# Gates spread over the partitions by way of DRAM, and an output projection begun earlier, in a two-layer diffusion step

## Chip, cores and metric

The kernel runs on one core of a Trainium2 chip. The metric is the device time of one execution in microseconds (us). Engines are named as in the profile: PE is TensorE (PEld its weight load), DVE VectorE, ACT ScalarE, POOL GpSimd, SP SyncE, which here only issues DMAs. A trailing q (SPq, ACTq, POOLq) is an engine's DMA issue.

## What is computed

One step of a trunk of two layers over 128 context and 512 latent tokens of width 1024. Layer 0 mixes with gated grouped-query attention, layer 1 with a bidirectional gated linear recurrence of 8 heads (HGRN2). Both end in an output projection, an adaLN gate and a LayerNorm:

```
mod = silu(cond) @ ada_w[i] + ada_b[i];  shift, scale, g = split(mod, 3)    # one set for context, one for latent tokens
h = x * (1 + scale) + shift
if i == 0: out = gated attention(h) @ attn_w_out
else:      out = (rms_norm(o) * norm_gain * silu(gate path)) @ rec_w_out     # o from the two scans of the recurrence
x = layer_norm(ALPHA * x + g * out, ln_gain[i], ln_bias[i])
```

Here g is one vector of 1024 numbers for the context tokens and one for the latent tokens, in each layer. Outputs are both token streams, the new key and value cache, and the recurrence's final states.

## The kernel before

*Numbers.* Most projections split each fp32 operand into two fp32r parts, hi and lo, and sum three products (hi·hi, hi·lo, lo·hi). A weight comes in pieces of 128x1024 (512 KB). `split_piece` makes hi by an ACT cast (L218) and lo by a subtraction (L219), here mostly on DVE. The raw pieces come through a ring of three buffers that SP loads in the order of the list `order` (L207); SP works in order, so a load that waits for a buffer holds those behind it.

*Stages.* Layer 0's attention takes the time to about 360 us. A scheduler (`weave`, with a timeline of its own) interleaves score and softmax blocks (`sc`, `pscp`, `p`, `pt`, `pot`) with side work: query projections (`qmm`, `qps`), and the adaLN products (`ada_gen`). For each chunk of 256 columns of ada_w, `ada_mms` sums over two raw pieces on PE (tile `adaps`, L261), DVE copies the row (L267), `ada_out` turns it into columns by four small matmuls (L275), and DVE adds the bias (L282). For a gate chunk that gives the tile `gcol`. `spread` then puts it on all partitions: four fp32 matmuls of a column, repeated along the free axis, against the identity (L291, tile `gateps`, eight instructions in the trace), and a DVE copy (L292) into `gate[layer]`. There are four such chunks for each layer. Layer 0's are spread as they come; layer 1's columns wait in `gcol1` for the tail. Then come layer 0's output projection (weights `attn_w_out`) and LayerNorm.

*Layer 1*, from about 440 us on: for head h, `proj_gen` projects v and g (`vgps`) and then q and the two forget gates (three groups `rps`, L1108 to L1110), while a `Lane` interleaves `gla_gen` of the head before, by due times. `gla_gen` runs seven levels (tile `lv`, L1238 and L1244; DVE products L1247 and L1252 and ACT copies `kc` L1216 and `near` L1254 between them), then `kp`, `sp`, `op`, a normalization (L1309 to L1315), the transposes `oT` (L1320) and the split of the head's output into `ghi` (ACT, L1321) and `glo` (DVE, L1322). POOL carries `x1a`, layer 0's output with gain and bias, as the residual.

*Tail.* After the last projection `tail_gen` is woven with the last head's `gla_gen` by `SIDE_T`: it splits the 8 pieces of rec_w_out one by one (order `OUT1`: both column halves nh of piece 0, then of piece 1, and so on), spreads one gate chunk for each pair, and begins output tiles 0 and 1 with the heads k that are done. `out_mms` makes three matmuls 128x512 for each token tile, half and k, 240 in all (tile `outp`, L993 to L995). `Norm` then finishes each of the 5 token tiles: y = outp·gate (L1013, reads a half as soon as it is complete), residual (L1014), statistics (L1015, L1020), 1/sqrt on POOL (L189), and two passes with gain and bias (L1029, L1030), each half stored on SP or ACT. Both halves of a tile lie in one pair of banks, so the first matmul of half 1 of a tile that was not begun early is held until DVE has read half 0.

Of the kernel before, what the change touches and what calls it, by code (L numbers as in the profile page):

```python
# [18 lines left out]
P = 128  # L19
# [112 lines left out]
def hybrid_step(ctx: ExitStack, tc: tile.TileContext, a: dict, o: dict):  # L132
# [137 lines left out]
    def ada_out(layer, c, row):  # L270

        part, c4 = divmod(c, 4)
        ps = bank1("adaps2")
        for j in range(2):
            nc.tensor.matmul(ps[:, 2 * j:2 * j + 2], row[:, j * P:(j + 1) * P], sel, start=True, stop=True)  # L275
        src = ps[:, :4].rearrange("p (a b) -> p a b", a=2)
        bias = view(adab, (layer * 3 + part) * KT + 2 * c4, [[1, 2], [0, 2]])
        if part < 2:
            nc.vector.tensor_tensor(shsc[layer][:, part, 2 * c4:2 * c4 + 2, :], src, bias, ALU.add)
            return None  # L280
        gcol = gcol1[:, c4] if layer else tiny.tile([P, 2, 2], F32, tag="gc", name="gcol")[:]
        nc.vector.tensor_tensor(gcol, src, bias, ALU.add)  # L282
        return None if layer else lambda: spread(layer, c4, gcol)

    def spread(layer, c4, gcol):

        ps = bank1("gateps")
        for s in range(2):
            for j in range(2):
                col = bass.AP(gcol.tensor, gcol.offset + 2 * j + s, [list(gcol.ap[0]), [0, P]])  # L290
                nc.tensor.matmul(ps[:, (2 * s + j) * P:(2 * s + j + 1) * P], col, ident, start=True, stop=True)  # L291
        nc.vector.tensor_copy(gate[layer][:, :, c4 * CW:(c4 + 1) * CW], ps[:].rearrange("p (a b) -> p a b", a=2))  # L292

    def ada_gen(chunks):
        todo, last = None, None
        for l, c in chunks:
            ps = bank1("adaps")
            ada_mms(ps, l, c, 0)
            ada_mms(ps, l, c, 1)
            if last:  # L300
                last()
            last = todo and ada_out(*todo)
            yield
            todo = (l, c, ada_row(ps))
        if last:
            last()
        if todo:
            last = ada_out(*todo)
            yield
            if last:  # L310
                last()
                yield

# [659 lines left out]
    weave(att, side, SIDE_B)  # L973
    side.finish()
    modA, modB = h1_mod()
    ph.close()
# [12 lines left out]
    def out_mms(ps, tt, nh, ghi, glo, ks=range(KT)):  # L989
        t = slice(tt * P, (tt + 1) * P)  # L990
        for k in ks:
            hi, lo = wo[nh, k // 2]
            nc.tensor.matmul(ps[:, nh, :], ghi[:, k, t], hi[:, k % 2, :], start=(k == 0), stop=False)  # L993
            nc.tensor.matmul(ps[:, nh, :], ghi[:, k, t], lo[:, k % 2, :], start=False, stop=False)  # L994
            nc.tensor.matmul(ps[:, nh, :], glo[:, k, t], hi[:, k % 2, :], start=False, stop=(k == KT - 1))  # L995

    class Norm:
        def __init__(self, layer, tt, ps=None):
            self.layer, self.tt = layer, tt
            self.ps = bank2("outp") if ps is None else ps  # L1000
            if layer == 0:
# [7 lines left out]
        def half(self, nh):  # L1009
            s = slice(nh * 512, (nh + 1) * 512)  # L1010
            y = self.y[:, s]
            g = gate[self.layer][:, 1 if self.tt == TS else 0, s]
            nc.vector.tensor_tensor(y, self.ps[:, nh, :], g, ALU.mult)  # L1013
            nc.vector.scalar_tensor_tensor(y, self.x[:, s], ALPHA, y, ALU.mult, ALU.add)  # L1014
            nc.vector.bn_stats(self.st[:, nh, :], y)  # L1015
# [47 lines left out]
    def proj_gen(h, H, first):  # L1063
# [94 lines left out]
        tiles()  # L1158
        evac_vg()
        for i in range(3):  # L1160
# [165 lines left out]
    class Residual:  # L1326
# [19 lines left out]
        def step(self):  # L1346
# [6 lines left out]
            for _ in range(2):  # L1353
                if self.todo and not (self.live and self.todo[0][1] == 0):
                    self.load(*self.todo.popleft())

    residual = Residual()
    for h in range(RH):
# [8 lines left out]

    outs = {}

    def tail_gen():  # L1370

        gate[1] = g2.tile([P, 2, D], F32, tag="A", name="gate1")
        w1 = gsp.tile([P, 2, 1024], F32R, tag="gate", name="w1")
        slots = [w1[:, i, :] for i in range(2)]
        for _ in range(2):
            slots += [wr.tile([P, 1024], F32R, tag=t, name=t)[:] for t in ("whi", "wlo")]
        for tt in range(2):
            outs[tt] = bank2("outp")
        for n, (nh, i) in enumerate(OUT1):
            if n == 3:  # L1380
                w2 = gsp.tile([P, 5, 1024], F32R, tag="gs", name="w2")
                w3 = h1p.tile([P, 5, 1024], F32R, tag="h1lo", name="w3")
                slots += [t[:, i, :] for t in (w2, w3) for i in range(5)]
            hi, lo = slots[2 * n], slots[2 * n + 1]
            wo[nh, i] = tuple(t.rearrange("p (k n) -> p k n", k=2) for t in (hi, lo))
            split_piece(hi, lo, ("rec_w_out", nh, i), nc.vector)
            yield
            if nh == 0:
                continue
            spread(1, i, gcol1[:, i])  # L1390
            yield
            for tt in range(2):
                for k in (2 * i, 2 * i + 1)[:2 if i < 3 else 1]:
                    for nh in range(2):
                        out_mms(outs[tt], tt, nh, ghi, glo, [k])
                    yield

    xp = lpool("xp", 3)
# [18 lines left out]
    for tt in range(TT):  # L1417
        norm = Norm(1, tt, outs.get(tt))
        for nh in range(2):
# [81 lines left out]
```

## Time and profile before

| | us |
|---|---|
| runs | 887.34, 887.74, 892.66 (median 887.74) |
| the profiled execution | 883.77, of which the span is 881.9 |
| PE busy in the span | 837.9 (95%) |
| DVE, ACT, POOL busy | 538.7, 374.1, 203.1 |
| last rps matmul begins | 789.24 |
| last outp matmul begins | 871.80 |

A row of the timeline gives start, length, engine, line, operation, out<-in, shape and count; the bracket is the idle time of the engine before it and what ended that. The windows give busy time and (xcount) for PE, PEld, DVE, ACT and POOL, then the granted PE clock, the DMA engines' busy share and GB/s. The rows on DMAs end with the KB of one and the median time from issue to landing. In a chain row, the middle number is the row's share of the path.

### The profile page before, as it was taken

What the parts mean: (1) busy time and instruction counts of PE and PEld (TensorE: products, weight loads), DVE (VectorE), ACT (ScalarE), POOL (GpSimd) and SP (SyncE); (2) the same over time, 40 slices, a digit from 0 to 9 for tenths busy, and PEclk for the clock granted to TensorE, in tenths of its full rate; (3) what the DMA queues carried; (4) which work ended last, traced back from release to release, by engine and by line L of the source; (5) the groups of instructions that cost most, each with busy time, mean ns of one, the idle gap of its engine ahead of it and who ended that gap; (6) DMA issues with size and microseconds to landing.
All of it is one profiled execution on the core that took longest, in us unless ns stands there. A gap on an engine that the chain in (4) does not pass through costs nothing.

```text
span 881.9 us, 19250 instructions
## 1 busy us (share of the span) xinstructions
PE 837.9 (95%) x8116; PEld 744.0 (84%) x8116; DVE 538.7 (61%) x972; ACT 374.1 (42%) x735; POOL 203.1 (23%) x250
## 2 busy tenths in 40 slices
PE   5999999989999998999999999999999999989995
PEld 3689998878878766788899999999999999987783
DVE  2456534664645657576437486676767585758495
ACT  2133536534554767422343453544434444444200
POOL 2013001422323733010000223243333224110110
PEclk9999999999999999999999999999999999998998
DMA  9922122143141136441131323231322323132121
GB/s 312 371 88 84 49 71 74 49 144 97 49 145 49 49 122 213 145 142 72 37 117 50 109 73 97 64 123 51 103 85 85 97 70 102 53 113 100 55 96 71
DMA packets 32678, 89.86 MB, mean 102 GB/s; under 512 B 4400, under 2 KB 11568, under 8 KB 32592
## 3 DMA queue, kind: packets, MB, share of 16 engines
q1 hardware_dynamic: 21984, 71.57, 24.6%
q0 software_dynamic: 3984, 12.13, 5.0%
q10 hardware_dynamic: 6624, 4.93, 1.8%
q8 instruction: 64, 1.05, 0.5%
q14 instruction: 22, 0.18, 0.1%
HBM read 79.44 MB, written 9.18 MB: 100 GB/s over the span
## 4 chain that ended last, share of the span: by engine, by line
PE 86%; DVE 4%; DMA 4%; ACT 2%; issue 1%; POOL 0%; SPq 0%; DVEq 0%; ACTq 0%; POOLq 0%
PE rps L1108 7%; PE rps L1109 6%; PE rps L1110 6%; PE vgps L1098 5%; PE vgps L1099 4%; PE vgps L1100 4%; PE outp L993 4%; PE outp L994 4%; PE outp L995 4%; PE pot L750 4%; PE pt L832 3%; PE adaps L261 2%; PE lv L1238 2%; PE gps L317 2%; PE gps L318 2%; PE gps L319 2%
## 5 line engine op out<-in xcount | busy, mean ns | idle before, releaser
L1108 PE MATMUL rps<-h1hi,rhi 128*128 128x320 f32 x368 | 118.2, 321 | 0.0
L1109 PE MATMUL rps<-h1lo,rhi 128*128 128x320 f32 x368 | 115.0, 312 | 0.0
L1110 PE MATMUL rps<-h1hi,rlo 128*128 128x320 f32 x368 | 113.9, 310 | 0.0
L825 POOL TENSOR_SCALAR p<-p,rc 128x640 f32<-128x640 f32 x64 | 53.4, 838 | 79.3 <-DVE rc L824 77.5
L1108 PEld LDWEIGHTS rps<-h1hi,rhi 128*128 128x128 f32 x368 | 69.8, 190 | 1.3
L1109 PEld LDWEIGHTS rps<-h1lo,rhi 128*128 128x128 f32 x368 | 69.3, 188 | 0.0
L1110 PEld LDWEIGHTS rps<-h1hi,rlo 128*128 128x128 f32 x368 | 69.3, 188 | 0.0
L219 DVE TENSOR_TENSOR rlo<-raw,rhi 128x1024 fp32r<-128x1024 f32 x32 | 46.0, 1441 | 34.3 <-ACT rhi L218 34.3
L820 ACT ACTIVATE p<-sc,nm 128x640 f32<-128x640 f32 x64 | 51.0, 799 | 30.9 <-DVE nm L817 23.2
L817 DVE TENSOR_REDUCE nm<-sc 128x1 f32<-128x640 f32 x64 | 52.1, 818 | 17.1 <-PE sc L724 16.7
L1266 POOL COPY At<-near 32x160 f32<-32x160 f32 x32 | 14.0, 438 | 198.1 <-DVE near L1228 197.1
L1216 ACT COPY kc<-A 128x640 f32<-128x640 f32 x40 | 32.1, 804 | 57.4 <-DVE A L1247 50.3
L218 ACT CAST rhi<-raw 128x1024 fp32r<-128x1024 f32 x32 | 33.5, 1048 | 50.5 <-PE rps L1109 47.6
L1098 PE MATMUL vgps<-rhi,h1hi 128*128 128x256 f32 x180 | 51.5, 286 | 1.2 <-ACT h1hi L948 1.2
L832 PE MATMUL pt<-small,p 128*128 128x128 f32 x320 | 49.1, 278 | 2.6 <-ACT pts L728 0.8
L1100 PE MATMUL vgps<-rhi,h1lo 128*128 128x256 f32 x180 | 50.9, 283 | 0.4 <-DVE h1lo L949 0.4
L1099 PE MATMUL vgps<-rlo,h1hi 128*128 128x256 f32 x180 | 50.9, 283 | 0.0
L728 ACT COPY pts<-pt 128x512 f32<-128x512 f32 x64 | 36.4, 586 | 28.2 <-PE pt L832 27.4
L723 PE MATMUL sc<-kk,X 128*128 128x320 f32 x128 | 43.0, 345 | 3.8 <-ACT p L820 3.3
L832 PEld LDWEIGHTS pt<-small,p 128*128 128x128 f32 x320 | 37.5, 143 | 8.2 <-issue 5.5
L1098 PE MATMUL vgps<-wspare,h1hi 128*128 128x256 f32 x140 | 41.7, 298 | 0.0
L317 PE MATMUL gps<-hhi,whi 128*128 128x320 f32 x128 | 40.0, 313 | 0.4 <-ACT X L576 0.4
(263 smaller groups left out, 2401.4 us busy)
## 6 DMA issues: line engine op xcount, KB each, us to landing
raw<-in_ada_w SPq DMA_DIRECT2D x48, 512.0 KB, 4.8
raw<-in_rec_w_in SPq DMA_DIRECT2D x40, 512.0 KB, 3.7
raw<-in_attn_w_in SPq DMA_DIRECT2D x16, 512.0 KB, 4.5
raw<-in_attn_w_out SPq DMA_DIRECT2D x8, 512.0 KB, 4.5
raw<-in_rec_w_out SPq DMA_DIRECT2D x8, 512.0 KB, 3.6
x1d<-y SPq DMA_DIRECT2D x5, 512.0 KB, 2.6
rx<-x1d POOLq DMA_DIRECT2D x20, 128.0 KB, 3.8
x1a<-rx POOLq DMA_DIRECT2D x20, 128.0 KB, 2.8
```

Of the source, the lines that this page charges most:

```text
L219: (lo_eng or nc.gpsimd).tensor_tensor(lo, raw, hi.bitcast(F32), ALU.subtract)
L317: nc.tensor.matmul(ps[:, :320], w.hi(k)[:, c], hhi[:, k, t], start=(k == 0), stop=False)
L817: nc.vector.tensor_reduce(nm[:, 0:1], sc[:, :, :320], AX.XY, ALU.max, negate=True)
L820: nc.scalar.activation(halves(p[:]), sc[:, :, :320], AF.Exp, bias=nm[:, 0:1], accum_out=su[:, 0:1])
L825: nc.gpsimd.tensor_scalar(p, p, rs[:, 0:1], 1.0, ALU.mult, ALU.mult)
L832: nc.tensor.transpose(pt[:, i * 256 + q * P:i * 256 + (q + 1) * P], ps[q][:, (k0 + i) * P:(k0 + i + 1) * P], ident)
L1098: nc.tensor.matmul(out, h1hi[:, k, t], hi, start=(k == 0), stop=False)
L1099: nc.tensor.matmul(out, h1hi[:, k, t], lo, start=False, stop=False)
L1100: nc.tensor.matmul(out, h1lo[:, k, t], hi, start=False, stop=(k == KT - 1))
L1108: nc.tensor.matmul(ps[:, j, :320], hi[:, k, :], h1hi[:, k, t], start=(k == 0), stop=False)
L1109: nc.tensor.matmul(ps[:, j, :320], hi[:, k, :], h1lo[:, k, t], start=False, stop=False)
L1110: nc.tensor.matmul(ps[:, j, :320], lo[:, k, :], h1hi[:, k, t], start=False, stop=(k == KT - 1))
```

## The change

1. The gate columns of both layers stay in `gcol[layer]`. `gate_rows` writes them as two rows of 1024 numbers to DRAM, and `load_gate` loads each row onto all 128 partitions (512 KB each). Layer 0: written after the second query unit, loaded in the third, on SP. Layer 1: written on SP after attention, loaded on POOL's queue ahead of the residual tiles. All `spread` matmuls and their DVE copies are gone.
2. `order` has the first piece of rec_w_out ahead of the last piece of rec_w_in. `Tail.split` splits the first two pieces inside the last head's projection, and tiles 0 and 1 take k = 0 and 1 of half 0 right behind its last rps matmul.
3. The rest of the tail follows the list `PLAN`, one entry for each step of the last head's `gla_gen`: "s" is a split, (tt, k) are both halves of tile tt with head k. Tile 2 is begun early too.
4. `out_mms` and `Norm` take a list with a view for each half; tiles 3 and 4 use two separate bank pairs, one for each half.

```diff
-    gcol1 = const.tile([P, 4, 2, 2], F32, name="gcol1")
+    gcol = [const.tile([P, KT, 2], F32, name=f"gcol{i}") for i in range(2)]
...
-        gcol = gcol1[:, c4] if layer else tiny.tile([P, 2, 2], F32, tag="gc", name="gcol")[:]
-        nc.vector.tensor_tensor(gcol, src, bias, ALU.add)
-        return None if layer else lambda: spread(layer, c4, gcol)
-
-    def spread(layer, c4, gcol):
-
-        ps = bank1("gateps")
+            return
+        nc.vector.tensor_tensor(gcol[layer][:, 2 * c4:2 * c4 + 2, :], src, bias, ALU.add)
+
+    def gate_rows(layer):
+
         for s in range(2):
-            for j in range(2):
-                col = bass.AP(gcol.tensor, gcol.offset + 2 * j + s, [list(gcol.ap[0]), [0, P]])
-                nc.tensor.matmul(ps[:, (2 * s + j) * P:(2 * s + j + 1) * P], col, ident, start=True, stop=True)
-        nc.vector.tensor_copy(gate[layer][:, :, c4 * CW:(c4 + 1) * CW], ps[:].rearrange("p (a b) -> p a b", a=2))
+            nc.sync.dma_start(gated[layer][s].rearrange("(k p) -> p k", p=P), gcol[layer][:, :, s])
+
+    def load_gate(layer, queue):
+        for s in range(2):
+            queue.dma_start(gate[layer][:, s, :], gated[layer][s:s + 1, :].to_broadcast((P, D)))
...
+    gated = [dram.tile([2, D], F32, name=f"gated{i}") for i in range(2)]
...
-    order.extend(("rec_w_out", nh, i) for nh, i in OUT1)
+    order.insert(len(order) - 1, ("rec_w_out", *OUT1[0]))
+    order.extend(("rec_w_out", nh, i) for nh, i in OUT1[1:])
...
         yield from q_gen(c, Xs[c], ada_gen(ADA_B[c - 1]))
+        if c == 1:
+            gate_rows(0)
+        elif c == 2:
+            load_gate(0, nc.sync)
...
     side.finish()
+    gate_rows(1)
...
+            ps = bank2("outp") if ps is None else ps
+            self.ps = [ps[:, 0, :], ps[:, 1, :]] if not isinstance(ps, list) else ps
...
         for i in range(3):
+            if last and i == 2:
+                tail.split()
             if i:
                 load_q(i)
             yield from mms(i, 0)
+            if last and i == 2:
+                tail.split()
             yield from mms(i, 1)
+            if last and i == 2:
+                tail.fill(0, 0, (0, 1))
+                tail.fill(1, 0, (0, 1))
             evac(i)
...
+        def fill(self, tt, nh, ks):
+            if tt not in self.outs:
+                ps = bank2("outp")
+                self.outs[tt] = [ps[:, 0, :], ps[:, 1, :]]
+            out_mms(self.outs[tt], tt, nh, ghi, glo, ks)
...
+    PLAN = (["s"], [(0, 2), "s"], [(1, 2), "s"], [(0, 3), (1, 3), "s"], [(0, 4), "s"], [(1, 4), (0, 5)], [(1, 5)],
+            [(0, 6), (1, 6)], [(2, 0)], [(2, 1), (2, 2)], [(2, 3), (2, 4), (2, 5), (2, 6)])
...
     for tt in range(3):
         load_resid(tt)
-    side = Side(("t", tail_gen()))
-    weave(lane.gens[0][0], side, SIDE_T)
-    side.finish()
+    gate[1] = g2.tile([P, 2, D], F32, tag="A", name="gate1")
+    load_gate(1, nc.gpsimd)
+    for tt in range(2):
+        tail.fill(tt, 1, (0, 1))
+    tail.split()
+    last = lane.gens[0][0]
+    for jobs in PLAN:
+        next(last)
+        for job in jobs:
+            if job == "s":
+                tail.split()
+            else:
+                tt, k = job
+                for nh in range(2):
+                    tail.fill(tt, nh, (k,))
+    drain(last)
+    outs = tail.outs
...
-        norm = Norm(1, tt, outs.get(tt))
+        norm = Norm(1, tt, outs.get(tt) or [bank2("outp")[:, 0, :] for _ in range(2)])
```

On SP, inside the attention block, these are the loads around the end of the attention's input weights, before and after (`gcol_78` holds layer 0's gate columns, `gated_90` its rows in DRAM, `gate_106` the rows on all partitions):

```order
L207 DMA raw<-in_attn_w_in 128x1024 [waits DMAHW6_49,DMAHW5_49,DVE_49]
L207 DMA raw<-in_ada_w 128x1024 [waits DMAHW7_49,DMAHW3_49,PE_49]
L207 DMA raw<-in_ada_w 128x1024 [waits DMAHW4_49,PE_49]
L207 DMA raw<-in_ada_w 128x1024 [waits DMAHW6_49,DVE_49]
L207 DMA raw<-in_ada_w 128x1024 [waits DMAHW7_49,PE_49]
```

```order
L207 DMA raw<-in_attn_w_in 128x1024 [waits DMAHW6_49,DMAHW5_49,DVE_49]
L286 DMA gated_90<-gcol_78 128x8x1 [waits DMAHW7_49,DVE_49]
L286 DMA gated_90<-gcol_78 128x8x1
L207 DMA raw<-in_ada_w 128x1024 [waits DMAHW3_49,PE_49]
L207 DMA raw<-in_ada_w 128x1024 [waits DMAHW4_49,PE_49]
L207 DMA raw<-in_ada_w 128x1024 [waits DMAHW6_49,Activation_49]
L290 DMA gate_106<-gated_90 128x1024 [waits DMAHW7_49]
L290 DMA gate_106<-gated_90 128x1024 [waits DMAHW0_49]
```

The two row writes, which wait for the last gate column, now stand between the attention's weights and the next ada_w, and the two loads of the rows three pieces later.

On PE, from the last rps matmul to the first level of the last head, before and after (after, `w_9280` and `whi`/`wlo` hold the first two split pieces of rec_w_out):

```order
L1110 MATMUL rps<-h1hi,rlo 128x320
L1320 MATMUL oT<-small,on 128x128 [waits DVE_49,Activation_49]
L1320 MATMUL oT<-small,on 128x128 [waits Activation_49] x4
L1238 MATMUL lv<-A,kc 32x32 [waits Activation_49]
L1238 MATMUL lv<-A,kc 32x32 x19
L291 MATMUL gateps<-small,gcol_78 128x128 x4
L993 MATMUL outp<-w_9412,ghi 128x512 [waits PE_49]
```

```order
L994 MATMUL outp<-w_9280,glo 128x512
L1328 MATMUL oT<-small,on 128x128 [waits DVE_49,Activation_49]
L1328 MATMUL oT<-small,on 128x128 x4
L992 MATMUL outp<-whi,ghi 128x512
L993 MATMUL outp<-wlo,ghi 128x512
L994 MATMUL outp<-whi,glo 128x512
```

After, twelve outp matmuls (the last of them is the first row) come between the last rps matmul and head 6's oT, and twelve more between that and the first lv group. From there on the outp matmuls stand in groups between the levels as before, without gateps; ahead of head 7's oT there are 126 of them, where there were 84.

On DVE, at the end of the program, after (`y` of the last half of the last tile is the third row; `x_9865` is tile 3, `x_9893` tile 4):

```order
L1014 SCALAR_TENSOR_TENSOR y<-x_9893,y 128x512 [waits DMASW0_49,DVE_49]
L1020 BN_AGGR mv<-st 128x2 [waits DVE_49]
L1013 TENSOR_TENSOR y<-outp,gate_9413 128x512 [waits PE_49]
L188 TENSOR_SCALAR rs_t<-mv 128x1 [waits DVE_49]
L1029 SCALAR_TENSOR_TENSOR x_9865<-y,mv,ln_9836 128x512 [waits DMAHW1_49,DMAHW0_49]
L1029 SCALAR_TENSOR_TENSOR x_9865<-y,mv,ln_9836 128x512
L1030 SCALAR_TENSOR_TENSOR x_9865<-x_9865,rstdl,ln_9836 128x512 [waits DVE_49,Pool_49]
L1030 SCALAR_TENSOR_TENSOR x_9865<-x_9865,rstdl,ln_9836 128x512 [waits DVE_49]
L1015 BN_STATS st<-y 128x6
```

The product for the last tile's second half, which waits for the last outp matmul, stood behind tile 3's last L1030 before; now it stands ahead of tile 3's two L1029 and two L1030.

More of the change, by code (lines that the diff above doesn't have):

```diff
@@ L992, in out_mms @@
             hi, lo = wo[nh, k // 2]
[L993 to L995 removed]
+            nc.tensor.matmul(ps[nh], ghi[:, k, t], hi[:, k % 2, :], start=(k == 0), stop=False)
+            nc.tensor.matmul(ps[nh], ghi[:, k, t], lo[:, k % 2, :], start=False, stop=False)
+            nc.tensor.matmul(ps[nh], glo[:, k, t], hi[:, k % 2, :], start=False, stop=(k == KT - 1))
     class Norm:
@@ L1159, in proj_gen @@
         evac_vg()
+        last = h == RH - 1
         for i in range(3):
+            if last and i == 2:
+                tail.split()
             if i:
@@ L1355, in step, with __init__, split @@
                     self.load(*self.todo.popleft())
+    class Tail:
+        def __init__(self):
+            self.outs, self.slots, self.n = {}, [], 0
+        def split(self):
+            n = self.n
+            if n == 0:
+                w = gsp.tile([P, 2, 1024], F32R, tag="gate", name="w1")
+                self.slots += [w[:, i, :] for i in range(2)]
+            elif n < 3:
+                self.slots += [wr.tile([P, 1024], F32R, tag=t, name=t)[:] for t in ("whi", "wlo")]
+            elif n == 3:
+                w2 = gsp.tile([P, 5, 1024], F32R, tag="gs", name="w2")
+                w3 = h1p.tile([P, 5, 1024], F32R, tag="h1lo", name="w3")
+                self.slots += [t[:, i, :] for t in (w2, w3) for i in range(5)]
+            self.n += 1
+            nh, i = OUT1[n]
+            hi, lo = self.slots[2 * n], self.slots[2 * n + 1]
+            wo[nh, i] = tuple(t.rearrange("p (k n) -> p k n", k=2) for t in (hi, lo))
+            split_piece(hi, lo, ("rec_w_out", nh, i), nc.vector)
+        def fill(self, tt, nh, ks):
[3 more added lines that the diff above has]
+            out_mms(self.outs[tt], tt, nh, ghi, glo, ks)
+    tail = Tail()
     residual = Residual()
@@ L1365, in hybrid_step @@
     lane.finish(1)
[L1368 to L1396, printed above, removed]
+    PLAN = (["s"], [(0, 2), "s"], [(1, 2), "s"], [(0, 3), (1, 3), "s"], [(0, 4), "s"], [(1, 4), (0, 5)], [(1, 5)],
+            [(0, 6), (1, 6)], [(2, 0)], [(2, 1), (2, 2)], [(2, 3), (2, 4), (2, 5), (2, 6)])
     xp = lpool("xp", 3)
```

18 lines of the change are left out of this document (5 added, 13 removed).

## The prediction

> **What bounds the kernel now.** First the page: busy times, then the chain that ended last.
>
> ```profile
> span 881.9 us, 19250 instructions
> PE 837.9 (95%) x8116; PEld 744.0 (84%) x8116; DVE 538.7 (61%) x972; ACT 374.1 (42%) x735; POOL 203.1 (23%) x250
> PE 86%; DVE 4%; DMA 4%; ACT 2%; issue 1%; POOL 0%; SPq 0%; DVEq 0%; ACTq 0%; POOLq 0%
> ```
>
> TensorE (PE) bounds the span, so an edit gains by taking PE work away or by filling PE's idle time. I then read the windows of the last head's recurrence and the output (start:end, length, busy time and count of PE, PEld, DVE, ACT, POOL, then PE's clock, the DMA share, GB/s):
>
> ```profile
> 786.00:797.00 11.00, 6.12 (x75) 5.58 (x74) 7.96 (x11) 7.94 (x18) 2.84 (x4) 0.78 0.58 203
> 820.00:836.00 16.00, 14.39 (x90) 12.02 (x89) 5.04 (x11) 3.50 (x14) 1.20 (x1) 1.00 0.24 75
> 845.00:860.00 15.00, 15.00 (x66) 12.02 (x65) 12.96 (x24) 0.00 (x0) 3.14 (x4) 1.00 0.41 141
> 860.00:872.00 12.00, 10.72 (x46) 8.20 (x44) 7.09 (x12) 0.00 (x0) 0.94 (x1) 1.00 0.23 87
> ```
>
> PE is half idle after 786. From 845 to 860 it is full, and 15.00 us are about 64.5 whole output matmuls: 0.233 us for one. The timeline has the idle stretches in brackets, with what ended them:
>
> ```profile
> 789.24 0.31 PE L1110 MATMUL rps<-h1hi,rlo 128*128 128x320 f32 x1
> 790.98 0.74 PE L1320 MATMUL oT<-small,on 128*128 128x128 f32 x5 [1.43 <-DVE on L1315]
> 795.16 0.77 PE L1238 MATMUL lv<-A,kc 128*32 128x32 f32 x40 [3.44 <-ACT kc L1216]
> 795.85 2.08 PE L291 MATMUL gateps<-small,gcol 128*128 128x128 f32 x8
> 800.43 0.55 PE L1238 MATMUL lv<-A,kc 128*32 128x32 f32 x40 [0.29 <-DVE A L1252]
> 833.27 0.74 PE L1320 MATMUL oT<-small,on 128*128 128x128 f32 x5 [1.61 <-DVE on L1315]
> 866.37 0.50 PE L993 MATMUL outp<-whi,ghi 128*128 128x512 f32 x1 [1.28 <-DVE y L1013]
> 872.23 0.69 DVE L1013 TENSOR_TENSOR y<-outp,gate 128x512 f32<-128x512 f32 x1 [4.46 <-PE outp L995]
> 876.08 1.41 DVE L1030 SCALAR_TENSOR_TENSOR x<-x,rstdl,ln 128x512 f32<-128x512 f32 x2
> ```
>
> From the last projection (789.55) to the last output matmul (872.2) PE idles 1.43 + 3.44 + 0.29 + 1.61 + 1.28 = 8.05 us. VectorE (DVE) then closes the kernel alone: 872.23 to 877.49.
>
> **The change, part by part: the tail.** The chain in order of time gives the gate copies there:
>
> ```profile
> 791.99 5.48 DMA raw<-in_rec_w_out
> 809.55 1.09 PE gateps L291 x8
> 817.62 1.09 PE gateps L291 x8
> 827.96 0.91 PE gateps L291 x8
> ```
>
> *Removed.* With the first group, which holds PE for about 1.73 us, the layer-1 `spread` groups cost 1.73 + 1.09 + 1.09 + 0.91 = 4.8 us of PE.
>
> *Moved.* 24 output matmuls (24 × 0.233 = 5.6 us) now stand around head 6's oT, where PE idled 1.43 and 3.44 us. The chain of head 7's levels hardly moves: its second level waited for a raw piece through cast, near, kc and the product at L1252, and that raw load still waits for the last split of the projection, so I keep 800.4. By the new order the levels, kp, sp, op and oT come out at about the same places as before (oT near 833.4), but 126 output matmuls stand ahead of oT instead of 84: 42 × 0.233 = 9.8 us done earlier, and 114 × 0.233 = 26.6 us are left behind it. Idle that stays: 0.8 at the second level, about 3 between the last levels and kp (fewer matmuls are put there), 0.9 for ghi, in all 4.7 us. So PE ends by one count at 872.2 − 4.8 − (8.05 − 4.7) − 0.5 (the first output matmuls ran slow after the idle stretch) = 863.5, by the other at 833.4 + 0.4 + 0.9 + 26.6 = 861.3. I take 862.5.
>
> Then DVE:
>
> ```profile
> 836.60 1.29 DVE L1013 TENSOR_TENSOR y<-outp,gate 128x512 f32<-128x512 f32 x2 [0.84 <-PE outp L995]
> 853.17 1.40 DVE L1013 TENSOR_TENSOR y<-outp,gate 128x512 f32<-128x512 f32 x2 [1.89 <-PE outp L995]
> 858.49 1.41 DVE L1030 SCALAR_TENSOR_TENSOR x<-x,rstdl,ln 128x512 f32<-128x512 f32 x2
> ```
>
> A tile holds DVE from 853.17 to 859.90, 6.73 us. Five of them from 836.60 on end at 870.25; DVE, with no slack left, is the next bound. The new order also puts tile 3's normalization (two L1029, two L1030: 2.65 us) and one L1015 (0.6) behind the last tile's y, so by PE's end it is 862.5 + 5.3 + 3.25 = 871.05. Before it was 877.49. Gain of the tail: 6.4 by the one, 7.2 by the other. **I take 6.5**, with bounds 4.5 (PE at 863.5 and one microsecond lost to the gate rows' 1 MB, which POOL issues just ahead of the residual loads) and 8.2 (PE at 861.3, an earlier start of DVE). The two banks for tiles 3 and 4 take away the 1.28 us, counted in the 8.05. The removed DVE copies are not on the path.
>
> **The first half.** The layer-0 gates leave the attention block, where the rows are:
>
> ```profile
> 179.90 1.05 PE L291 MATMUL gateps<-small,gcol 128*128 128x128 f32 x8
> 191.09 1.04 ACT L218 CAST whi<-raw 128x1024 fp32r<-128x1024 f32 x1 [1.92 <-DMA raw<-in_attn_w_in]
> 191.49 12.03 SPq L207 DMA_DIRECT2D raw<-in_ada_w  x5
> 191.79 1.16 PE L291 MATMUL gateps<-small,gcol 128*128 128x128 f32 x8
> 194.64 1.84 PE L291 MATMUL gateps<-small,gcol 128*128 128x128 f32 x8 [0.25 <-DVE gcol L282]
> 197.12 0.41 DVE L567 TENSOR_TENSOR qs<-r,qs 128x256 fp32r<-128x256 f32 x1
> 197.66 2.08 PE L291 MATMUL gateps<-small,gcol 128*128 128x128 f32 x8 [0.54 <-DVE gcol L282]
> 201.01 1.41 PE L261 MATMUL adaps<-raw,sil 128*32 128x256 f32 x16
> 202.77 0.31 PE L723 MATMUL pscp<-kk,X 128*128 128x128 f32 x1
> ```
>
> The group at 179.90 buys nothing: a raw landing at 191.09 follows. The other three hold PE for some 4.3 us (their 5.08 less what overlaps the next matmuls). Without them PE comes sooner to the transposes of qs, which DVE has ready at 197.53, and to the products behind these, and waits: I keep about half, +2.0 at the point that PE reached at 204.04, with bounds 0 and 4.3. But SP, which issued ada_w at 191.49, now first waits for the last gate column (it came at 197.6, ahead of the group at 197.66; without the two groups before it, about 195.05) and writes two rows of 1024 elements, 4 bytes each. PE meets `adaps` soon after, in order, so this load's landing decides. Rows that price it:
>
> ```profile
> raw<-in_ada_w SPq DMA_DIRECT2D x48, 512.0 KB, 4.8
> S<-in_state ACTq DMA_DIRECT2D x16, 64.0 KB, 1.9
> ngain<-in_norm_gain ACTq DMA_DIRECT2D x1, 0.5 KB, 2.8
> q10 hardware_dynamic: 6624, 4.93, 1.8%
> 143.04 0.33 ACTq L911 DMA_DIRECT2D lbr<-in_lb  x1
> 143.41 0.45 ACTq L913 DMA_DIRECT2D lnc<-in_ln_c  x1
> ```
>
> Issue: lbr is 128 runs, lnc 256, so 0.12 us for 128 more, and a row of 1024 takes about 1.15. Transfer: the two rows are 128 packets on each of 16 engines. Low: the q10 queue spends 1.8% × 16 × 881.9 / 6624 = 38 ns a packet. High: ngain, 128 runs of 4 bytes, lands 0.9 us later than the 64 KB of S, 8 packets an engine: 0.11 us. The load behind them needs 3.3 us of its own (from S to ada_w 448 KB more take 2.9, so 512 KB take 3.3).
> - At no price for a packet: issued by 195.9, landed 200.7; the +2.0 stays.
> - At 38 ns: 196.2 + 4.9 + 3.3 = 204.4, then the adaps matmuls (1.3) and 0.9 for slow matmuls after the idle stretch (2.08 against 1.16 in the rows of L291): 206.6 against 204.04, **−2.5**.
> - At 0.11 us: 196.2 + 14.1 + 3.3 + 2.2 = 215.8, −11.8.
>
> I take 38 ns, measured over 6624 packets that are also small, against one load. The whole change breaks even where 196.2 + 128p + 5.5 = 204.04 + 6.5, at 69 ns. The two loads of the layer-0 rows (1 MB, SP) come three pieces later: the five ada_w issues there took 12.03 us because SP waited for buffers, so I cost the loads at nothing (6.6 us if PE waited for both in full). That gate is read only after attention. The layer-1 rows are written here:
>
> ```profile
> 361.49 2.00 ACT L218 CAST wohi<-raw 128x1024 fp32r<-128x1024 f32 x2 [2.33 <-PE pot L750]
> 341.78 4.47 SPq L207 DMA_DIRECT2D raw<-in_attn_w_out  x3
> ```
>
> The weights queued behind that write are issued from 341.78 to 346.25 and cast at 361.49: with 5 us for the load there are 10 us of cover, so I cost it at nothing (at 0.11 us, 14 us of packets would stick out by 4).
>
> The Trainium skill speaks against this write: "DMA: Bandwidth & Descriptors", § Rules for kernel authors, has a last dimension that is not contiguous lowered to one descriptor for each element. Its § Bandwidth gives a floor of about 10.5 ns a packet for loads of 4 KB; by that price, an estimate, the two rows take 1.3 us, the first half gains 1.0 and the sum is 7.5 (880.2, rival 1's side). No row here shows so low a price, and these are writes; the sum stays with the rows.
>
> The page "TensorE: Matmul & The Clock Gate", § Part 1: The HAM clock gate, of the Trainium skill halves the clock after about 3.4 us without work and for about as long again. The trace agrees (L291 at 2.08 after 3.44 of idle, at 1.16 elsewhere); by that rule a stall of 6 us here would cost an estimated 1.7, not 0.9, and the sum would be 0.8 lower.
>
> **Sum.** 6.5 − 2.5 = 4.0 us. The profiled execution took 883.77 (span 881.9): changed 879.8, span 877.9. The median of the runs shown is 887.74: 883.7.
>
> **Rivals.**
> 1. *The row write is cheap or hidden*: packets near 18 ns or less, or the engines take the raw load beside them. Then 6.5 + 2.0 = 8.5, 879.2; with the tail at its bound, 877.5. For it: 8 KB are little. Against: the writes stand ahead on the same queue, and lbr and lnc land late (3.2 and 4.2 us) for their 16 and 8 KB.
> 2. *Slower: the row write holds SP.* From 69 ns a packet on it eats the tail's gain; at 0.11 us PE waits at `adaps` until 213.6, −11.8 + 6.5 = −5.3: 893.0. For it: ngain, the nearest row in form (4-byte runs). Against: one small read, whose 0.9 us may be no packet time at all.
> 3. *Half the tail arrives*: the gate rows, the residual loads and the raws collide at 787 to 797 (DMA share already 0.58), the second level slips 2 to 3 us and the closing DVE chain with it. Gain 3.5 − 2.5 = 1.0: 886.7. Against: 24 matmuls now fill that wait.
>
> **How the numbers follow.** Chances: forecast 0.50 (883.7; its own range 881 to 886), rival 1 0.24, rival 2 0.14, rival 3 0.12. The range 877.5 to 891 reaches to rival 1's end and two thirds into rival 2. A measurement of this kernel can tell about 1%, 8.9 us, from no change. Faster by more (under 878.9): two thirds of rival 1 (0.16), and a fifth of the forecast's cases, where the three groups give 4.3 and the tail 8.2 (0.10): 0.26. Slower by more (over 896.6): 0.05 of rival 2, with packets over 0.11 us, and 0.03 for collisions in rival 3 that cost far more: 0.08. Within: 0.66.
>
> **What would show it.** Tail right: no L291, outp matmuls close around head 6's oT, some 73 us from the last rps matmul to the last outp matmul (82.65 before), and DVE nearly without gaps from tile 0 to the end. First half right: two `gated` issues of over 1 us on SP near 195 to 197, and PE idle for 3 to 6 us ahead of an `adaps` group, ended by DMA raw<-in_ada_w. No such idle time means rival 1; over 10 us means rival 2. A second `lv` group more than 12 us after the last rps matmul (10.9 before) means rival 3. I am wrong altogether if the output weights near 361 wait for the layer-1 rows, or if the block's new order moves PE's work elsewhere by more than these terms.

## The result, and the profile after

The changed kernel took 903.18 us (median of 4 runs, 899.05 to 906.51) against 888.42 before on the same chip: ratio 1.0156, interval 1.0127 to 1.0184. It is slower by about 14 us; 883.7 was forecast. The page after, busy times and the chain that ended last:

```profile
span 904.4 us, 19132 instructions
PE 840.2 (93%) x8052; PEld 745.1 (82%) x8052; DVE 534.0 (59%) x964; ACT 373.8 (41%) x735; POOL 203.2 (22%) x252
PE 84%; DMA 7%; DVE 4%; ACT 2%; issue 1%; SPq 0%; POOL 0%; DVEq 0%; ACTq 0%
```

DMA's share of the chain went from 4% to 7%. PE issued 64 matmul records fewer and was busy 2.3 us longer, so some of them ran slower. The windows cut at the same four places (start, the middle of attention, its last `pot`, the last projection, the end) say where; first before, then after:

```profile
0.00:160.00 160.00, 147.34 (x1040) 129.00 (x1042) 77.84 (x155) 61.42 (x108) 24.68 (x28) 1.00 0.44 149
160.00:362.00 202.00, 190.37 (x1575) 152.65 (x1574) 118.64 (x268) 114.26 (x249) 71.70 (x75) 0.98 0.30 97
362.00:789.00 427.00, 425.05 (x4870) 402.53 (x4871) 276.12 (x438) 180.05 (x344) 95.46 (x133) 1.00 0.30 90
789.00:882.00 93.00, 75.10 (x636) 59.87 (x634) 66.08 (x112) 18.38 (x36) 11.24 (x16) 0.92 0.26 87
```

```profile
0.00:160.00 160.00, 147.72 (x1035) 128.86 (x1036) 76.60 (x153) 60.75 (x107) 23.44 (x26) 1.00 0.43 146
160.00:388.00 228.00, 196.43 (x1548) 155.72 (x1546) 118.38 (x266) 114.43 (x249) 71.78 (x77) 0.91 0.33 92
388.00:815.00 427.00, 425.02 (x4871) 403.17 (x4871) 276.31 (x438) 180.51 (x344) 96.79 (x136) 1.00 0.30 91
815.00:904.00 89.00, 71.05 (x604) 57.40 (x602) 62.76 (x108) 18.09 (x36) 11.19 (x16) 0.91 0.27 99
```

The tail gained 4 us. The second half of attention lost 26: PE's idle time there grew from 11.6 to 31.6 us, and its work took 6 us longer at a mean clock of 0.91 in place of 0.98, although four `gateps` groups (about 6 us by their rows) no longer stand in it. The timeline of PE shows the waits, and the tail:

```profile
212.70 1.08 PE L261 MATMUL adaps<-raw,sil 128*32 128x256 f32 x8 [12.09 <-DMA raw<-in_ada_w]
351.92 1.08 PE L261 MATMUL adaps<-raw,sil 128*32 128x256 f32 x8 [2.86 <-DMA raw<-in_ada_w]
370.02 0.63 PE L717 MATMUL sc<-kk,X 128*128 128x320 f32 x1 [4.15 <-ACT p L814]
...
815.15 0.31 PE L1110 MATMUL rps<-h1hi,rlo 128*128 128x320 f32 x1
818.05 0.71 PE L1328 MATMUL oT<-small,on 128*128 128x128 f32 x5
821.44 0.63 PE L1246 MATMUL lv<-A,kc 128*32 128x32 f32 x40
827.64 0.55 PE L1246 MATMUL lv<-A,kc 128*32 128x32 f32 x40 [1.95 <-DVE A L1260]
863.43 0.71 PE L1328 MATMUL oT<-small,on 128*128 128x128 f32 x5
890.98 0.39 PE L994 MATMUL outp<-w,glo 128*128 128x512 f32 x1
```

Before, the three waits of attention were 0, at most 0.6, and 1.0 us. SP and the landing time of the row writes (last number of the second fence, median of four):

```profile
195.34 1.01 SPq L286 DMA_DIRECT2D gated<-gcol  x2
196.44 1.48 SPq L207 DMA_DIRECT2D raw<-in_ada_w  x3
206.01 3.95 SPq L290 DMA_DIRECT2D gate<-gated  x2
213.83 14.89 SPq L207 DMA_DIRECT2D raw<-in_ada_w  x4
```

```profile
gated<-gcol SPq DMA_DIRECT2D x4, 4.0 KB, 11.0
```

Two rows of 4 KB are issued in 1 us and take 11 us to land. The first gate load waits for the first row until 206.01, so that landed 10.7 us after its issue; the second took 13.7. The raw ada_w behind the rows, issued at 196.44, lands 16.1 us later, just before 212.70. The median load of that kind takes 4.8. The windows show that hardly any data moved while the rows were on their way (the last number is GB/s, the one before it the busy share of the DMA engines):

```profile
198.00:209.00 11.00, 2.61 (x11) 2.21 (x10) 2.19 (x5) 2.57 (x11) 1.82 (x2) 0.50 0.59 16
209.00:213.00 4.00, 0.30 (x4) 0.23 (x8) 0.00 (x0) 0.00 (x0) 0.00 (x0) 0.50 0.82 306
```

The small packets themselves are not the time: in the trace's packet records the 2048 of 4 bytes all begin between 196.2 and 197.6 and take 7 to 9 ns each. It is the 4096-byte packets of the load behind them that then take up to 5 us, where their median is 0.159.

### The profile page after: what moved, and what is told of

Same layout as the page of the kernel before. It is cut to its first block, busy times and chain, and to the rows that moved or that the text cites. A ratio compares the mean times of both kernels' runs of the same rounds, so it can differ in the third digit from the quotient of the medians.

```text
span 904.4 us, 19132 instructions
## 1 busy us (share of the span) xinstructions
PE 840.2 (93%) x8052; PEld 745.1 (82%) x8052; DVE 534.0 (59%) x964; ACT 373.8 (41%) x735; POOL 203.2 (22%) x252
## 3 DMA queue, kind: packets, MB, share of 16 engines
q10 hardware_dynamic: 6624, 4.93, 1.7%
## 4 chain that ended last, share of the span: by engine, by line
PE 84%; DMA 7%; DVE 4%; ACT 2%; issue 1%; SPq 0%; POOL 0%; DVEq 0%; ACTq 0%
PE rps L1108 7%; PE rps L1109 6%; PE rps L1110 6%; PE vgps L1098 5%; PE vgps L1100 4%; PE vgps L1099 4%; PE outp L992 4%; PE outp L994 4%; PE pot L744 4%; PE outp L993 4%; DMA raw<-in_ada_w 4%; PE pt L826 3%; PE adaps L261 3%; PE lv L1246 2%; PE gps L309 2%; PE gps L310 2%
## 5 line engine op out<-in xcount | busy, mean ns | idle before, releaser
L826 PE MATMUL pt<-small,p 128*128 128x128 f32 x320 | 52.4, 290 | 2.4 <-ACT pts L722 0.9
L261 PE MATMUL adaps<-raw,sil 128*32 128x256 f32 x384 | 31.3, 432 | 19.5 <-DMA raw<-in_ada_w 18.5
L826 PEld LDWEIGHTS pt<-small,p 128*128 128x128 f32 x320 | 39.9, 149 | 8.8 <-issue 4.7
```

The lines of the kernel that those rows point to most:

```text
L261: nc.tensor.matmul(ps[32 * q:32 * q + 32, :CW], sil[:, 4 * i + q, :], raw[:, q * CW:(q + 1) * CW], start=(i == 0), stop=(i == 1))
L826: nc.tensor.transpose(pt[:, i * 256 + q * P:i * 256 + (q + 1) * P], ps[q][:, (k0 + i) * P:(k0 + i + 1) * P], ident)
```

## The experiments

After the comparison of the traces the theory is that the 4-byte rows hold SP's loads. Its rivals are SP's wait for the last gate column, the block's new order, or the gate load in the tail. Where only one execution was timed, I read landing times and waits, not the total.

**runs32, runs32_l0: fewer and longer runs**

```diff
-    gcol = [const.tile([P, KT, 2], F32, ...
+    gcol = [const.tile([P, 2, KT], F32, ...
-            nc.sync.dma_start(gated[layer][s].rearrange("(k p) -> p k", p=P), gcol[layer][:, :, s])
+            nc.sync.dma_start(gated[layer][s].rearrange("(p k) -> p k", p=P), gcol[layer][:, s, :])   # runs32_l0: layer 0 alone
```

> Both layers' gate rows go to DRAM in 128 runs of 32 bytes a row in place of 1024 runs of 4 bytes (the gate columns are kept with the stream outermost, and the row is written partition by partition, so the gates arrive permuted and the two outputs are scaled by the wrong gates). Same bytes, same queue, same order. Theory (the number of packets on SP's rings holds the raw load behind them, about 0.1 us a packet on each engine): the idle time ahead of adaps near 201 falls from 12.1 us to under 2, the ACT cast near 368 waits under 1 us where it waited 5.1, attention ends 22 to 27 us earlier, and the time is 876 to 882. Rival (SP's wait for the last gate column, or the block's new order, costs the time, whatever the runs): the idle time stays over 8 us and the time over 895.

> The 32-byte runs for layer 0's rows alone; layer 1's rows stay in 4-byte runs (layer 0's gates arrive permuted). Theory that the two writes cost about 15 (layer 0) and 9.5 us (layer 1), one by one: 886 to 890, no stall near 201, and the ACT cast that waits for raw attn_w_out keeps its wait of 4 to 6 us. Rival that the late loss near 350 to 375 only follows from the loads having been late since 201: it goes as well, 876 to 882.

runs32 took 880.1 us (5 runs), ratio 0.9905 (0.9868 to 0.9943); runs32_l0 883.22 (6 runs), 0.9935 (0.9905 to 0.9964). Timeline of runs32, SP and PE, and its landing time:

```profile
193.77 0.81 SPq L286 DMA_DIRECT2D gated<-gcol  x2
194.67 1.33 SPq L207 DMA_DIRECT2D raw<-in_ada_w  x3
198.97 1.08 PE L261 MATMUL adaps<-raw,sil 128*32 128x256 f32 x8
```

```profile
gated<-gcol SPq DMA_DIRECT2D x4, 4.0 KB, 2.6
```

Same bytes, queue and order: the rows land in 2.6 us (layer 0's in 1.4 and 1.5), `adaps` waits for nothing, and 23 us are gone. So the runs cost the time, and SP's wait for the column does not. Layer 1's 4-byte rows alone are worth 3.1 us by the medians, with intervals that overlap; 9.5 was expected of them. I had read that off the changed kernel, where they met a block already late.

**rows_act: another queue.** `nc.scalar.dma_start` for the two row writes.

> The rows are written in 4-byte runs as in the change, but from ACT's queue (the loads of the rows stay on SP and POOL). If the small packets only stand ahead of the raw load in SP's own rings: the raw load goes out at once and shares the engines, the stall near 201 falls under 5 us, and the time is 880 to 888. If they hold the engines themselves (or what feeds both queues), the raw load is as late as before: stall 8 us or more, time over 896.

883.11 us (6 runs), ratio 0.9935 (0.9906 to 0.9964), in the range expected of a raw load that goes out at once. Its rows take longer to land than ever, and `adaps` does not wait at this place:

```profile
gated<-gcol ACTq DMA_DIRECT2D x4, 4.0 KB, 14.8
```

```profile
197.29 2.01 PE L261 MATMUL adaps<-raw,sil 128*32 128x256 f32 x16
```

That does not show that another queue is free of the delay. The ada_w pieces that PE meets here were issued from 192.84 on, ahead of the rows (194.84), since SP no longer waits for the gate column, and landed in time, after 4.0 to 4.9 us. SP issued two more, at 198.44 and 199.37. Their landing times, and the windows of rows_act around them:

```profile
DMA to landing us min/median/max: 14.8/15.0/15.1
```

```profile
196.00:199.00 3.00, 3.00 (x24) 1.37 (x23) 0.00 (x0) 1.17 (x2) 0.00 (x0) 0.50 1.03 364
199.00:210.00 11.00, 11.00 (x71) 10.77 (x68) 2.88 (x6) 2.68 (x10) 1.04 (x1) 0.71 1.11 34
210.00:213.00 3.00, 3.00 (x31) 2.72 (x29) 1.76 (x4) 2.12 (x5) 0.80 (x1) 1.00 0.83 221
```

While the rows are on their way, loads on the other queue are as late as in the changed kernel (16.1 us), and the DMA engines move 34 GB/s although they count as busy. Layer 1's rows, on ACT's queue from 346.95 on, did the same to three loads that SP issued from 347.49 to 353.10: they landed after 13.5 to 15.8 us. So the rows hold the engines, or what lies behind them, for both queues: the second of the two expectations in mechanism. The move helped by putting the load that PE needs ahead of the rows. By the next `pscp` group PE was 2.7 us behind the kernel before, where runs32 was level with it.

**late_gate: the tail's gate load moved**

```diff
-    load_gate(1, nc.gpsimd)
...
+    for n, jobs in enumerate(PLAN):
         next(last)
+        if n == 3:
+            load_gate(1, nc.gpsimd)
```

> The load of layer 1's gate rows (1 MB on POOL's queue) is issued after the fourth entry of PLAN, 18 us or more behind the last rps matmul, in place of ahead of the residual loads. Theory (the 1 MB delays the raw load that the second level waits for, and PE then runs at a lower clock): that load lands 5.5 us after its issue where it took 6.8, the second lv group begins about 10.9 us after the last rps matmul where it took 12.2, head 7's oT comes 4 us earlier, and the time falls by 2.5 to 4 us. Rival (the raw pieces and residual loads alone fill that stretch): under 1 us.

900.8 us (4 runs), ratio 1.0119 (1.008 to 1.0159), which overlaps the changed kernel's. In its execution the second level began 11.03 us after the last rps matmul ended (824.00 against 812.97), oT 43.78 after it, and DVE finished at 80.17; in the changed kernel 12.18, 47.97 and 84.36. That is what was expected. But seven other kernels (rows_act, and six below) kept the load early and also had the second level at 10.8 to 11.3, most with DVE's end at 79.9 to 80.5; runs16, runs32_l0 and runs32 had it at 11.5 to 11.9. The collision happened in the changed kernel's execution; that the early load causes it is not shown.

**half_l0, eighth_l0, src4: how the delay depends on the dose**

```diff
half_l0:   row 0 as in runs32, row 1 in 4-byte runs
eighth_l0: row 0 as in runs32; of row 1
+                nc.sync.dma_start(row[896:1024].rearrange("(k p) -> p k", p=P), col[:, 7:8])
+                nc.sync.dma_start(row[0:896].rearrange("(p k) -> p k", p=P), col[:, 0:7])
src4:      destination as in runs32, source columns as in the change (8 bytes apart)
```

> Of layer 0's two rows one is written in 4-byte runs and the other in 32-byte runs (its gates arrive permuted); layer 1's rows stay in 4-byte runs. Theory (about 0.1 us for each 4-byte packet on each engine): 64 packets an engine in place of 128 take 6 to 7 us less, so the idle time ahead of adaps near 201 is 4.5 to 6.5 us, half way between the 12.1 of the change and nearly none with 32-byte runs. Rival (one fixed delay that any such write brings): 10 us or more.

> Layer 0's rows are written in 32-byte and 28-byte runs but for one eighth of the second row, 128 numbers in 4-byte runs: 8 such packets on each engine in place of 128 (its gates arrive permuted). If the delay goes with the number of 4-byte packets: the idle time ahead of adaps near 200 is under 2 us. If one write of 4-byte runs brings a fixed delay, as half a dose with nearly the whole stall suggests: 8 us or more.

> The rows land in DRAM partition by partition, 32 contiguous bytes from each, but are read from the change's own gate columns, where a stream's numbers stand 8 bytes apart: 1024 source runs of 4 bytes a row, destination contiguous (the gates arrive permuted). If scattered 4-byte writes in DRAM are what takes the time: stall under 3 us, as with 32-byte runs. If the number of packets is: stall over 9 us, as in the change.

PE's wait in the timelines of half_l0, eighth_l0 and src4, in this order:

```profile
210.38 1.08 PE L261 MATMUL adaps<-raw,sil 128*32 128x256 f32 x8 [11.10 <-DMA raw<-in_ada_w]
```

```profile
208.55 1.08 PE L261 MATMUL adaps<-raw,sil 128*32 128x256 f32 x8 [7.90 <-DMA raw<-in_ada_w]
```

```profile
204.88 1.08 PE L261 MATMUL adaps<-raw,sil 128*32 128x256 f32 x8 [6.26 <-DMA raw<-in_ada_w]
```

(893.35, 896.85 and 895.15 us, one run each.) The theory of a price for each packet fell: 128, 64 and 8 packets of 4 bytes an engine gave 12.1, 11.1 and 7.9 us. And with src4 no guess held: contiguous rows in DRAM, still 6.3 us.

**extra4, extra4_wide, runs16: what makes a short write slow.** In all three layer 0's and 1's rows are in 32-byte runs, but for runs16.

```diff
extra4:
+            nc.sync.dma_start(spare[0:1, :].rearrange("a b -> b a"), gcol[0][:, 1, 7:8])   # behind layer 0's rows, side by side
extra4_wide:
+            nc.sync.dma_start(spare[:, 0:1], gcol[0][:, 1, 7:8])                           # 512 bytes apart
runs16: layer 0's rows in two writes each, four numbers from each partition
```

> Both layers' rows in 32-byte runs (gates permuted) and, right behind layer 0's, one more write of 128 numbers in 4-byte runs, side by side in DRAM, which nothing reads: 8 such packets on each engine. Theory of a fixed delay for a write of 4-byte runs: SP's ada_w lands some 8 us late, and the idle time ahead of adaps near 200 is 5 to 9 us. Rival (the 28-byte runs of the eighth, or the count, brought its delay): under 2 us.

> As extra4, but the 128 numbers of the additional write stand 512 bytes apart in DRAM. If neighbouring 4-byte writes get in each other's way: no stall (under 2 us). If each short write is slow for itself: as extra4.

> Layer 0's rows in 16-byte runs, two writes a row, half of them ahead of the last attn_w_in and half ahead of ada_w (gates permuted); layer 1's in 32-byte runs. If every run under 32 bytes is slow: a stall of 6 us or more ahead of adaps near 200, or a late attn_w_in. If only runs of 4 bytes are: under 2 us.

Landing times in extra4, extra4_wide and runs16:

```profile
spare<-gcol SPq DMA_DIRECT2D x1, 0.5 KB, 8.9
```

```profile
spare<-gcol SPq DMA_DIRECT2D x1, 0.5 KB, 1.5
```

```profile
gated<-gcol SPq DMA_DIRECT2D x4, 2.0 KB, 2.3
```

PE's waits were 5.1, 0.65 and 0.37 us (890.11, 889.87 and 883.23 us, one run each). 128 numbers of 4 bytes take 8.9 us to land side by side and 1.5 us when 512 bytes lie between them. Neither the count nor the length of a run decides alone; it matters how the writes lie in DRAM. The table has layer 0's writes alone, with one value for each write. The medians of `gated<-gcol` above also hold writes issued right behind a 512 KB load that was still under way, which took 3.0 to 3.9 us in runs32 and runs16:

| write | writes in one stretch of 512 bytes | landing, us |
|---|---|---|
| rows_act, 4-byte runs | 128 | 13.3, 14.8 |
| the change's rows, 4-byte runs | 128 | 10.7, 13.7 |
| late_gate, the same rows | 128 | 10.6, 12.4 |
| half_l0, the row in 4-byte runs | 128 | 12.1 |
| extra4 | 128 | 8.9 |
| eighth_l0's 128 numbers | 128 | 8.1 |
| src4 | 128 | 6.9, 8.1 |
| runs32 | 16 | 1.4, 1.5 |
| runs16, second halves | 16 | 1.4, 1.7 |
| extra4_wide | 1 | 1.5 |
| rows_pe (below), 512-byte runs | 1 | 1.4 |

The writes fall into two groups: 7 to 15 us where 128 short writes lie side by side, and 1.4 to 1.7 us for the rest. A fixed price for each neighbour does not fit: by (8.9 − 1.5) / 127 = 58 ns, 16 neighbours would land after 2.4 us, and they landed as soon as single writes. The whole row, with eight times the writes, took 4 us longer than its eighth (half_l0 against eighth_l0). Where between 16 and 128 the delay begins, and whether it goes by the number of neighbours, by their distance or by a length under 16 bytes together with one of these, no run tells; nor is the width of 512 bytes measured. The Trainium skill, "DMA: Bandwidth & Descriptors", § Specifications, has transfers below 512 bytes done by read-modify-write. No run here shows what the engines do with a write; a reading by which every write below 512 bytes is slow does not fit, since runs of 16 and 32 bytes, and 4-byte writes 512 bytes apart, landed in 1.4 to 1.7 us.

**rows_pe, rows_pe_moved, one_bank, rows_act_late, tail_only: whole versions, with all gates in their places**

```diff
rows_pe:
+        ps = bank1("growps")
+        nc.tensor.transpose(ps[:2 * KT, :P], gcol[layer][:].rearrange("p s k -> p (s k)"), ident)
+        row = rowp.tile([P, CW], F32, tag="row", name="grow")[:2 * KT, :P]
+        nc.vector.tensor_copy(row, ps[:2 * KT, :P])
+        nc.sync.dma_start(gated[layer][:].rearrange("s (k p) -> (s k) p", p=P), row)
rows_pe_moved: and gate_rows(0), load_gate(0) one query unit later; gate_rows(1) behind the output weights; late_gate's move
one_bank: rows_pe_moved with
+        norm = Norm(1, tt, outs.get(tt))
rows_act_late: rows_pe_moved with the rows written from nc.scalar, load_gate(0, nc.sync) behind the block
tail_only: layer 0 with spread as before the change, layer 1 as rows_pe_moved
```

> The gate columns are turned by one PE transpose into 16 rows of 128 numbers, copied by DVE, and written in 16 runs of 512 bytes; all else as in the change. Theory (the runs are what costs): as with 32-byte runs, 876 to 882, with no stall near 201. Rival (the transpose, its copy and SP's wait for them cost as much as the runs): over 890.

> As rows_pe, and three moves: layer 0's rows are written after the third query unit (loaded after the fourth), layer 1's after the output weights are loaded, and layer 1's gate load is issued after the fourth entry of PLAN. Theory (SP's wait for the last gate column holds the loads behind it, 2 us at the end of attention; the gate load delays the second level, 2 to 4 us): 872 to 877. Rival (the loads there have slack, the tail ends with DVE in any case): 878 to 882, as rows_pe.

> As rows_pe_moved, but tiles 3 and 4 have one pair of banks each, as before the change. Theory (PE waits again for DVE's read of half 0, and PE's end still counts): 1 to 3 us slower than rows_pe_moved, with a wait of outp on DVE y of over 1 us in the last 30 us. Rival (DVE closes the kernel back to back whatever PE does): the same within 1 us.

> The tail of the change alone: layer 0's gates are spread by PE as before the change; layer 1's rows are written in 512-byte runs after the output weights and loaded in the tail after the fourth entry of PLAN. Theory (the tail gives 6 to 8 us where no raw is held up, and the detour by DRAM in the attention block gives nothing): 878 to 882, the attention block within 1 us of before. Rival (half the tail's gain, as in the changed kernel's profile): 883 to 885.

> The best of the parts for gates by way of DRAM: one PE transpose, 512-byte runs, the rows written from ACT's queue, layer 0's load on SP behind the following chunk's pieces, layer 1's gate load late in the tail. If SP's order alone made the detour cost 2 to 4 us in attention: the 3 us that the three spread groups gave near 200 stay to the end, 875 to 879. If the 1 MB load itself holds an ada_w piece wherever it stands: 880 to 884.

| kernel | us (runs) | ratio to before, interval |
|---|---|---|
| rows_pe | 883.29 (10) | 0.9941, 0.9918 to 0.9964 |
| rows_pe_moved | 883.19 (12) | 0.9935, 0.9913 to 0.9957 |
| one_bank | 882.83 (9) | 0.9947, 0.9922 to 0.9972 |
| rows_act_late | 880.03 (6) | 0.9912, 0.9894 to 0.993 |
| tail_only | 877.11 (6) | 0.989, 0.9861 to 0.9918 |

rows_pe missed its 876 to 882 by 1 us. The three moves gave nothing, where I had expected some 5 us. In rows_pe_moved PE was 3.2 us ahead of before until about 239, as the three missing groups allow, and behind it by 2.0 at 316, after the row write and the 1 MB load (issued at 253 to 256) had passed through SP; that these two cost it is not shown. rows_act_late came out at the lower end of its second expectation (880 to 884). The detour by DRAM showed no gain in any form with the gates in their places: the best of them, rows_act_late, does not differ clearly from tail_only, which does without it for layer 0.

tail_only is the version that beats both the kernel before and the change: 1.1% faster than before. It leaves layer 0's gates on PE. Its time is a little below the 878 to 882 expected, but its attention block was not within 1 us of before: in the profiled execution (881.47 us, one of its slower ones) the first outp matmul came 2.9 us later behind the first `pot`. In one_bank PE lost what was expected of it, and the time did not follow; waits of PE in its last 100 us:

```profile
PE outp L994 <- DVE y L1015: 3.0, 1, 3.0
```

Its last outp matmul came 3.7 us later behind the last rps matmul than in rows_pe_moved, and DVE's end 0.7: DVE closes the kernel back to back.

## Why the prediction was wrong, step by step

- **The row write's price: the step that failed.** "I take 38 ns, measured over 6624 packets" made −2.5 of what was −14.7 by the next `pscp` group (at 260.92 before; from the first `pot` 101.1 us before, 115.8 after). No packet price was the right form: the rows landed after 10.7 and 13.7 us, the load behind them after 16.1, and PE idled 12.1 us at `adaps`, while the 4-byte packets took 7 to 9 ns each. The 6624 packets behind my 38 ns carry 744 bytes on the average (4.93 MB), so they are no row for a 4-byte write. Between eighth_l0 and the change, 120 packets an engine more took 4.2 us, 35 ns each, near my figure; the working lacked the 8 us of the first 128 neighbouring writes, which no write of the trace before had shown. The issue was misread too: I took 1.15 us for one row, and the two took 1.01 together; the ada_w left at 196.44, near the working's 196.2 (195.05 + 1.15, one issue for two rows).
- **Rival 2** named the place, the waiting instruction and the size: PE held at `adaps` until 213.6, measured 212.70. Its price of 0.11 us a packet was right by chance, and 0.14 was too small a chance for the nearest row in form.
- **Layer 1's rows "at nothing"** failed as well. I gave them the cast at 361.49 as their first reader. The piece ahead of it is cast in the midst of the softmax, by ACT in order; its load, issued at 358.64, 1.1 us ahead of the row write, took until about 368 (9.5 us). This load stands ahead of the rows, so no order in SP's queue explains its delay; that the rows hold the DMA engines for all loads, as in rows_act, would. ACT in the changed kernel:

```profile
368.14 1.04 ACT L218 CAST wohi<-raw 128x1024 fp32r<-128x1024 f32 x1 [5.06 <-DMA raw<-in_attn_w_out]
```

  PE's 4.15 us at 370.02 follow from it. By the medians layer 1's rows cost 3 us where nothing else is late (runs32_l0 against runs32, with intervals that overlap). From that `pscp` group to the first outp matmul the changed kernel lost 10.1 us; kernels with the same layer-1 rows and a stall lost 3.4 (half_l0) and 7.7 (late_gate, eighth_l0), and runs32, without slow rows, 2.1. In runs32_l0 the same piece, issued 0.8 us ahead of the same write, was there after 4.7 us. What decides within this spread is open.
- **The clock** had 0.9 us in the sum. From 351 to 388 the granted clock was 0.82, from 213 to 218 it was 0.50 (0.97 from 218 to 222): 37 × 0.18 + 5 × 0.50 = 9 us of full-speed time, an upper figure, since PE also idled there and the block before had a mean of 0.98. The Trainium skill, "TensorE: Matmul & The Clock Gate", § Part 1: The HAM clock gate, gave the rule that made the sum 0.8 lower. It was nearer: by it an estimate of 1.7 for the first stall, and 213 to 218 alone show 5 × 0.50 = 2.5. The agreement that I read off the rows before was too quick, though: L291 also took 2.08 at 197.66, after 0.54 us of idle time, where the granted clock was 0.50 (197 to 200, before).
- **The +2.0 from the three groups** was about right at its point (in runs32 the `qmm` matmuls stood 1.5 to 2.9 us earlier where the kernel before is at 204 to 210) and did not last: less than 0.1 was left by the next `pscp` group. What paces the block by then was not looked for.
- **The tail: mechanism right.** No L291, matmuls close around oT, 126 ahead of head 7's oT. PE's end 75.9 us after the last rps matmul (72.95 forecast, 82.65 before); DVE's end 84.4 (81.5 forecast, 87.9 before), so 3.6 in place of 6.5 in this execution. The second level stood at 12.18, the sign of rival 3; after its 1.95 us of idle time the clock fell (0.50 from 829.5 to 832.5), and the third level came 6.2 us behind it (4.1 before). In half_l0, rows_pe, rows_act, eighth_l0, src4 and extra4, with the same tail, DVE ended at 79.9 to 80.5: 7.5 to 8.0 gained; in runs16, runs32, extra4_wide and runs32_l0 at 80.6 to 83.6: 4.4 to 7.3. So the forecast of 6.5 lies inside the spread of one tail, 3.6 to 8.0. tail_only's median is 10 us under that of before, more than the tail gave in any of these executions; where the rest comes from is open.
- **DVE as the next bound**: right. Its end follows the y of tile 0 by 33.1 us (33.65 forecast), shown here by the first and the last row of the stretch, and one_bank confirms it:

```profile
866.72 1.29 DVE L1013 TENSOR_TENSOR y<-outp,gate 128x512 f32<-128x512 f32 x2 [0.83 <-PE outp L994]
...
898.41 1.41 DVE L1030 SCALAR_TENSOR_TENSOR x<-x,rstdl,ln 128x512 f32<-128x512 f32 x2
```

## What to carry to other kernels

A write whose price no row shows is bounded by a write, not by a read, and its bound must hold a fixed part besides the count. A DMA of many 4-byte writes side by side delays the loads around it, on its own queue (16.1 us here) and on another (14.8): give it longer runs (rows of 512 bytes landed in 1.4 us), or issue it where no load that something waits for is near. When a change has two independent parts, price and build them apart: here one part hid a gain of 1.1% (tail_only) behind a loss of 2.7% (the change against tail_only).

## What the runs showed of the hardware that I had not expected

- 128 writes of 4 bytes to neighbouring addresses in DRAM took 8.9 us to land, the same writes 512 bytes apart 1.5 us (one execution each); 1024 of them took 10.6 to 14.8 (6.9 and 8.1 where eight neighbours came from one partition, src4), and 16-byte and 32-byte runs 1.4 to 1.7.
- Such a write delays loads on its own queue (16.1 us to landing, where the median is 4.8) and on another (14.8 and 15.1); the DMA engines then moved 16 and 34 GB/s at a busy share of 0.59 and 1.11.
- The wait of 12 us was followed by 5 us at a granted clock of 0.50, and in a block already late the shorter waits behind it went with 37 us at 0.82.
